# Trainium2, one core: several edits at the end of a retrieval kernel — an earlier fence, a tile of its own, half of a one-hot build on VectorE, the last rows by halves

## The chip, the cores and the metric

One NeuronCore of one Trainium2 chip runs the whole program. Its engines are named here as in the profile: PE is TensorE (matmuls), PEld its weight loads, DVE is VectorE, ACT is ScalarE, POOL is GpSimd, and SP is SyncE, which here only issues DMAs. Each engine works through its own instructions in the order in which the program gives them, and waits on semaphores for the others. The metric is the device time of one execution in microseconds (us). The time of the kernel before is the median of three executions; the profile is of one further execution.

## The reference

The program is one step of one decoder layer, for 512 prompt tokens and 32 sample tokens of width 1024. A mixer (retention heads beside a convolution) and a layer norm come first; they are not touched by the change. Then comes a product-key expert layer, and a last layer norm:

```python
q = (xb @ w_query).reshape(PEER_BLOCK, PEER_HEADS, PEER_DQ)          # 8 heads
s1 = jnp.einsum('phd,hkd->phk', q1, sub_keys_1)                      # 128 keys each
...
idx = e1 * N_KEYS + e2                                               # 16 of 16384 experts per head
gate = jax.nn.softmax(sv.astype(jnp.float32), axis=-1)
u = jnp.take(peer_u, idx, axis=0)
act = jax.nn.gelu(jnp.einsum('phkd,pd->phk', u, xb), approximate=False)
vv = jnp.take(peer_v, idx, axis=0)
return jnp.einsum('phk,phkd->pd', gate * act, vv)
...
x = layer_norm(ALPHA * x + ffn, ln2_g, ln2_b)
```

Each token thus picks 8 x 16 = 128 experts out of 16384. An expert is a row of peer_u and a row of peer_v, 1024 numbers each in float32.

## The kernel before

The 544 tokens are ordered as chunk 0 (128 prompt tokens), 32 sample tokens ("s"), chunk "b" (128 prompt tokens), and 256 prompt tokens that remain. The expert layer is done in two ways at the same time.

**By gathering** (chunk 0, then "s", then "b"). `gather`, lines 582 to 605, runs over slots. For each slot POOL issues an indirect DMA that brings 128 expert rows (8 KB each, 1 MB in all) into a buffer `g` (line 587); DVE multiplies the first half of each row with the token's x1 and sums it up, which is the *dot* (line 590); ACT applies the gelu and the gate (lines 598 and 599); DVE adds the weighted second half to `acc` (line 604). Chunk 0 and chunk "b" have 128 slots each. "s" packs four heads' shares of its 32 tokens onto 128 partitions and has 32 slots. The buffers `g` come from a pool of three, and in the slots with k % 4 == 3 of a long chunk from one more pool. `finish` (line 607) adds the scaled x1, applies the last norm and writes the chunk out, over SP's queue. `x1g`, the tile with the x1 of the chunk at hand, is one buffer that "s" and "b" use in turn (line 1006); it is loaded over ACT's queue from a copy in DRAM.

**Densely** (the other 256 tokens, `ND`). Here every expert is computed. The 16384 experts are sorted into 128 *keys* of 128 experts (the key is e2, the place within it e1). For a key, `scores_of` (line 808) loads 512 KB of peer_u over SP into a buffer `uv` (a pool of four) and makes 128 experts x 256 tokens of scores with eight matmuls, 16 records of line 815 in the profile. The gelu of them is multiplied by a gate matrix G. `v_products` (line 927) then multiplies G by a 512 KB row block of peer_v, which `v_row` (line 922) loads into the same four buffers: for each half `b` of the 256 tokens two matmuls into the two PSUM banks pB[b][0] and pB[b][1], four records of line 930 per half and row. `v_stage` (line 966) is one row for both halves.

The gate matrices are built from one-hot matrices in `build` (line 886), in units of TB = 8 tokens, 32 units in a pass. For a unit ACT makes A, which is 1 where e1 equals the row number: eight instructions that take the absolute difference (`off`, line 893) and one that takes relu(1 - x) (line 895). DVE makes M, the same comparison for e2 (line 897), and the products B of M with the gates in three bf16 parts (line 901). PE multiplies A by B, 24 matmuls per unit (line 906). A, M and B have two buffers each. The first pass (`first_keys`, line 934) builds keys 0 to 95 in groups of four tokens, and DVE multiplies the result into the scores that stand there already, or copies it where the scores come later (lines 945 and 947). The second pass (`last_keys`, line 959) builds keys 96 to 127 in groups of 16 tokens, which ACT copies out (line 963). Its target Gd takes the room of Gb, so that it can't be written before rows 0 to 31 are done.

**The order.** A planner puts the instructions of each engine in an order, by simulating them: earlier in the program text means higher priority, but an instruction that is ready is taken before one that isn't. `behind(ins, other)` (line 166) adds an order between two instructions of one engine. The following are set by hand around the change:

- In `first_keys` eight rows (`AHEAD`) are loaded and used for the first half, each behind the matmuls of a later group of tokens (`marks`).
- `first_keys` returns its last multiply; it is the *fence* (line 1019). Dots of "s" from slot FREE = 20 on, and all dots of "b", stand behind it on DVE (line 595).
- `run` (line 1021) takes one step of `phases` and two slots of `fetched` in turn. `phases` (line 971) does the second half of rows 4 to 7, which are still in their buffers, then of rows 0 to 3, which it loads again, then rows 8 to 31, the second pass with rows from 32 on, the scores of the last keys in between, and the rows up to 123. The last four rows are loaded together; line 995 does all of them for half 0 and then for half 1, in the program text. No `behind` holds this order.
- At the end two layer norms read the halves from PSUM (line 1024).

Of the kernel before, what the change touches and what calls it, by code (L numbers as in the profile page):

```python
# [8 lines left out]
F32 = mybir.dt.float32  # L9
F32R = mybir.dt.float32r  # L10
BF = mybir.dt.bfloat16
# [3 lines left out]
AF = mybir.ActivationFunctionType  # L15
# [79 lines left out]
def tile_step(ctx: ExitStack, tc: tile.TileContext, a, o):  # L95
# [508 lines left out]
                V.scalar_tensor_tensor(acc, v, wgt, acc, op0=OP.mult, op1=OP.add)  # L604
            yield

    def finish(x1, f, n, dsts, t, table=False):

        for q in range(2):
            c = slice(q * 512, (q + 1) * 512)  # L610
            V.scalar_tensor_tensor(t[:n, c], x1[:n, c], ALPHA, f[q][:n], op0=OP.mult, op1=OP.add)
        layer_norm(t, n, ln2[0], ln2[1], table=table)
        for p0, p1, dst in dsts:
            nc.sync.dma_start(dst, t[p0:p1])

    def run(*gens):

# [19 lines left out]
        Ig[g] = per.tile([128, PH // r_ * TK], I32, name=f"I{g}")  # L637
    e1T = per.tile([128, ND], F32, name="e1T")
    e2T = per.tile([128, ND], BF, name="e2T")
    gtT = per.tile([128, 3, ND], BF, name="gtT")  # L640


# [193 lines left out]
    for g in range(2):  # L836
        ef = eg[:, g].rearrange("p h k -> p (h k)")
        ei = rp.tile([128, 128], I32, name="ei")
        V.tensor_copy(ei, ef)
        V.tensor_scalar(ei, ei, NK - 1, None, op0=OP.bitwise_and)  # L840
        e1 = rp.tile([128, 128], F32, name="e1")
        V.tensor_copy(e1, ei)
        e2 = rp.tile([128, 128], F32, name="e2")
        V.tensor_sub(e2, ef, e1)
        V.tensor_scalar(e2, e2, 1.0 / NK, None, op0=OP.mult)
        p = mmps().rearrange("p (q t) -> p q t", q=4)
        for q, t in enumerate((e1, e2, eg[:, 2 + g].rearrange("p h k -> p (h k)"))):
            T.transpose(p[:, q], t, ident)
        gr = rp.tile([128, 128], F32, name="e2")
        S.activation(gr, p[:, 2], AF.Copy)  # L850
        cs = slice(g * 128, (g + 1) * 128)
        S.activation(e1T[:, cs], p[:, 0], AF.Copy, scale=-1.0)
        S.activation(e2T[:, cs], p[:, 1], AF.Copy)
        for q in range(3):
            V.tensor_copy(gtT[:, q, cs], gr)
            if q < 2:
                V.tensor_sub(gr, gr, gtT[:, q, cs])
# [28 lines left out]
    def build(bt, e0, ne, nt):  # L886


        pt = None
        for t1 in range(0, ND, TB):  # L890
            off = bt.tile([128, TB, NK], BF, name="off", bufs=1)
            for t in range(TB):
                S.activation(off[:, t], row, AF.Abs, bias=e1T[:, t1 + t:t1 + t + 1])  # L893
            A = bt.tile([128, TB, NK], BF, name="A")
            S.activation(A, off, AF.Relu, bias=1.0, scale=-1.0)  # L895
            M = bt.tile([128, TB // 2, ne, 2], BF, name="M")
            V.tensor_tensor(M, iot[:, e0:e0 + ne].unsqueeze(1).to_broadcast([128, TB // 2, ne, 2]),
                            pairs_of(e2T, t1).to_broadcast([128, TB // 2, ne, 2]), op=OP.is_equal)
            B = bt.tile([128, 3, TB // 2, ne, 2], BF, name="B")
            for q in range(3):  # L900
                V.tensor_tensor(B[:, q], M, pairs_of(gtT[:, q], t1).to_broadcast([128, TB // 2, ne, 2]), op=OP.mult)  # L901
            for t in range(t1, t1 + TB):
                if t % nt == 0:
                    pt = pdn.tile([128, nt, ne], F32, name="mm")
                for q in range(3):
                    mm = T.matmul(pt[:, t % nt], A[:, t - t1], B[:, q, (t - t1) // 2, :, t % 2], start=(q == 0),  # L906
                                  stop=(q == 2))
                if t % nt == nt - 1:
                    yield pt, slice(t - nt + 1, t + 1), mm
# [24 lines left out]
    def first_keys():  # L934

        with tc.tile_pool(name="bt", bufs=2, reuse_waits="tile") as bt:
            done = 0
            for pt, ts, mm in build(bt, 0, E0S[3], 4):
                for g, e0, e1, ready in ((0, 0, EG[0], True), (2, 0, EG[2], True), (1, 0, done, True), (1, done, EG[1], False)):
                    if e0 == e1:  # L940
                        continue
                    to = GW[g][:, e0:e1, ts]
                    part = pt[:, :, E0S[g] + e0:E0S[g] + e1].rearrange("p t e -> p e t")
                    if ready:
                        last = V.tensor_mul(to, to, part)
                    else:
                        V.tensor_copy(to, part)  # L947
                if ts.stop % 12 == 0 and done < EG[1]:
                    s_stage(E0S[1] + done, ts.stop)
                    done += 1  # L950
                if ts.stop >= 192 and ts.stop % 8 == 0:
                    marks.append(mm)
            for mm in marks[:AHEAD]:
                ahead.append(v_row(len(ahead)))
                for p in v_products(len(ahead) - 1, ahead[-1], 0):
                    behind(p, mm)
        return last

    def last_keys():

# [8 lines left out]
            v_products(e, vt, b)  # L969

    def phases():
        for e in [*range(AHEAD - UV, AHEAD), *range(AHEAD - UV)]:
            v_products(e, ahead[e] if e >= AHEAD - UV else v_row(e), 1)
            yield
        for e in range(len(ahead), EG[0]):
            v_stage(e)
            yield
        gbs.close()
        gd = ctx.enter_context(tc.tile_pool(name="gd", bufs=1, side="right", reuse_waits="tile"))
# [14 lines left out]
        ends = [(e, v_row(e)) for e in range(NK - UV, NK)]  # L994
        for b in range(2):
            for e, vt in ends:
                v_products(e, vt, b)
                yield

    def fetched():  # L1000
        t = dn.tile([128, D], F32, name="yt")
        finish(x1_0, [acc0[:, 0:512], acc0[:, 512:]], 128, [(0, 128, o[0][0, 0:128])], t)
        yield
        for g, c0, dst in (("s", 0, o[1].rearrange("b i d -> (b i) d")), ("b", NS, o[0][0, 128:256])):
            w_, r_ = GSP[g]
# [68 lines left out]
```

## Time and profile before

| what | us |
|---|---|
| median of 3 executions (1558.17 to 1561.06) | 1560.78 |
| the profiled execution, whole time | 1557.44 |
| the profiled execution, span of the trace | 1555.7 |
| granted TensorE clock, mean | 0.983 |
| PE busy | 1484.1 |
| DVE busy | 1227.7 |
| ACT busy | 581.4 |
| POOL busy | 369.6 |

The span is the time from the first to the last instruction that the profiler saw. Times in the trace count from its start. A line such as L930 is a line of the kernel before; a name such as `pB<-uv,Gd` gives the tile that is written and those that are read. "Idle before" an instruction is the time in which its engine did nothing, and the arrow names what ended it. PE's matmuls are pipelined, and their ends are modelled: a busy PE may hold short waits, and these show at PEld, the weight loads. The trace moves 505.85 MB by DMA.

### The profile page before, as it was taken

Reading aid. Unit: us, or ns where it says so; the run is one execution under the profiler, and the core shown is the slowest. Engines: PE = TensorE matmul, PEld = TensorE weight load, DVE = VectorE, ACT = ScalarE, POOL = GpSimd, SP = SyncE. Lnnn points to the kernel's source line nnn. Section 1 sums busy time; section 2 is a strip of 40 time slices with the busy share of each in tenths; the row PEclk is TensorE's granted clock in tenths of the full one; section 3 lists DMA queues with packets and bytes.
Section 4 is the critical chain, followed back from the end, with each engine's and each line's share of the span. In section 5 each row is a group of like instructions: output and inputs, shape, how many; then the busy total and the mean of one; then the engine's idle time right before and its main releaser. Section 6 shows DMA issues by size and latency. Waiting matters only on the chain.

```text
span 1555.7 us, 20736 instructions
## 1 busy us (share of the span) xinstructions
PE 1484.1 (95%) x7046; PEld 1004.1 (65%) x7046; DVE 1227.7 (79%) x3151; ACT 581.4 (37%) x1633; POOL 369.6 (24%) x329
## 2 busy tenths in 40 slices
PE   6999999897999999999999999999999999999997
PEld 6978667565866668788888884444566555543333
DVE  4779998978747999999978988666777777766664
ACT  2224453125112333333534898426992111111110
POOL 2001225322312222312231101222223222322210
PEclk9999999998999999999999999999999999999999
DMA  9648787985688779999999624999999999999993
GB/s 362 243 153 353 252 297 257 347 334 206 226 339 341 273 260 363 358 330 346 366 382 360 240 88 177 394 350 402 347 372 394 423 424 424 424 424 424 424 410 121
DMA packets 100119, 505.85 MB, mean 325 GB/s; under 512 B 10247, under 2 KB 21255, under 8 KB 57125
## 3 DMA queue, kind: packets, MB, share of 16 engines
q0 software_dynamic: 42240, 305.12, 50.4%
q1 hardware_dynamic: 51325, 192.05, 32.4%
q10 hardware_dynamic: 6448, 7.36, 1.5%
q8 instruction: 55, 0.90, 0.2%
q14 instruction: 51, 0.42, 0.1%
HBM read 499.12 MB, written 5.80 MB: 325 GB/s over the span
## 4 chain that ended last, share of the span: by engine, by line
PE 55%; DVE 20%; DMA 12%; issue 9%; POOL 3%; ACT 2%; DVEq 0%; SPq 0%; POOLq 0%; ACTq 0%
PE pB L930 27%; PE sp L815 11%; DMA g<-in_uv_dram,I 6%; PE mm L199 5%; PE mm L486 5%; DVE acc L604 4%; DVE g L590 4%; PE mm L906 3%; POOL g L587 2%; DMA g<-in_uv_dram,Is 2%; DMA g<-in_w_in_dram 2%; DMA uv<-in_uv_dram 1%; PE mm L310 1%; DVE B L901 1%; DVE score L516 1%
## 5 line engine op out<-in xcount | busy, mean ns | idle before, releaser
L815 PE MATMUL sp<-x1T,uv 128*128 128x256 f32 x2048 | 464.1, 383 | 5.2 <-DMA uv<-in_ut_dram 2.8
L604 DVE SCALAR_TENSOR_TENSOR acc<-g,wgt,acc 128x1024 f32<-128x1024 f32 x285 | 364.5, 1279 | 102.0 <-ACT wgt L599 100.4
L815 PEld LDWEIGHTS sp<-x1T,uv 128*128 128x128 f32 x2048 | 384.7, 191 | 78.5 <-issue 28.2
L598 ACT ACTIVATE act<-act 128x1 f32<-128x1 f32 x288 | 57.8, 201 | 625.7 <-DVE g L590 625.4
L587 POOL DMA_INDIRECT g<-in_uv_dram,I x128 | 166.9, 1304 | 460.1 <-DVE acc L604 259.2
L590 DVE SCALAR_TENSOR_TENSOR g<-g,x1g 128x1024 f32<-128x1024 f32 x160 | 195.2, 1222 | 71.8 <-DMA g<-in_uv_dram,Ib 50.5
L587 POOL DMA_INDIRECT g<-in_uv_dram,Ib x128 | 140.6, 1098 | 442.0 <-DVE acc L604 293.7
L199 PE MATMUL mm<-x1T,w 128*128 128x384 f32 (+1 forms) x512 | 178.3, 504 | 1.5 <-ACT score L535 1.2
L590 DVE SCALAR_TENSOR_TENSOR g<-g,x 128x1024 f32<-128x1024 f32 x128 | 154.8, 1214 | 31.0 <-DMA g<-in_uv_dram,I 30.9
L930 PE MATMUL pB<-uv,Ga 128*128 128x512 f32 x352 | 162.1, 604 | 0.2
L893 ACT ACTIVATE off<-row,e1T 128x128 bf16<-128x128 bf16 x512 | 158.0, 388 | 1.0
L199 PEld LDWEIGHTS mm<-x1T,w 128*128 128x128 f32 x512 | 97.4, 192 | 73.7 <-issue 40.3
L930 PE MATMUL pB<-uv,Gb 128*128 128x512 f32 x256 | 113.5, 597 | 4.9 <-DMA uv<-in_uv_dram 4.5
L930 PEld LDWEIGHTS pB<-uv,Ga 128*128 128x128 f32 x352 | 63.7, 189 | 83.4 <-issue 63.1
L930 PE MATMUL pB<-uv,Gd 128*128 128x512 f32 x256 | 115.5, 599 | 0.8
L930 PEld LDWEIGHTS pB<-uv,Gd 128*128 128x128 f32 x256 | 46.7, 190 | 69.7 <-issue 69.5
L930 PEld LDWEIGHTS pB<-uv,Gb 128*128 128x128 f32 x256 | 47.4, 190 | 60.7 <-issue 52.9
L906 PEld LDWEIGHTS <-A 128*128 128x128 bf16 x1536 | 60.5, 96 | 31.3 <-issue 21.3
L901 DVE TENSOR_TENSOR B<-M,gtT 128x768 bf16<-128x768 bf16 (+1 forms) x192 | 69.4, 416 | 9.4 <-PE mm L906 9.2
L930 PE MATMUL pB<-uv,Gc 128*128 128x512 f32 x160 | 72.8, 600 | 0.0
L895 ACT ACTIVATE A<-off 128x1024 bf16<-128x1024 bf16 x64 | 67.4, 1053 | 9.3 <-PE mm L906 8.5
L906 PE MATMUL mm<-B,A 128*128 128x96 bf16 (+1 forms) x1536 | 63.9, 191 | 7.3 <-DVE Gc L947 6.5
(274 smaller groups left out, 1675.4 us busy)
## 6 DMA issues: line engine op xcount, KB each, us to landing
uv<-in_uv_dram SPq DMA_DIRECT2D x132, 512.0 KB
uv<-in_ut_dram SPq DMA_DIRECT2D x128, 512.0 KB
w<-in_w_in_dram SPq DMA_DIRECT2D x18, 1024.0 KB
w<-in_w_query_dram SPq DMA_DIRECT2D x16, 1024.0 KB
w<-in_w_out_dram SPq DMA_DIRECT2D x7, 1024.0 KB
g<-in_uv_dram,I POOLq DMA_INDIRECT x128
keys<-in_state_retention_dram ACTq DMA_DIRECT2D x4, 512.0 KB
out_dram<-keys SPq DMA_DIRECT2D x4, 512.0 KB
```

What stands on the lines that cost most here:

```text
L199: T.matmul(p[:, :n], w[m // 2][:, k, (m % 2) * 128:(m % 2 + 1) * 128], xT[:, k, c0:c0 + n], start=(k == 0), stop=(k == 7))
L486: last = T.matmul(banks_[q][:n, s * 256:(s + 1) * 256], src[:, k, c0:c0 + n], wo[q * 2 + s][:, k0 + k, :], start=(xT is None and k0 == 4 a ...
L587: G.indirect_dma_start(out=t, out_offset=None, in_=a["uv"], in_offset=bass.IndirectOffsetOnAxis(ap=idx[:, k:k + 1], axis=0))
L590: dot = V.scalar_tensor_tensor(t[:, :D], t[:, :D], 1.0, x1, op0=OP.mult, op1=OP.mult, accum_out=act[:, 0:1])
L598: S.activation(act[:, 1:2], act[:, 0:1], AF.Gelu)
L604: V.scalar_tensor_tensor(acc, v, wgt, acc, op0=OP.mult, op1=OP.add)
L815: T.matmul(sp[:, i], u[:, k], x1T[:, k, NG2:], start=(k == 0), stop=(k == 7), skip_group_check=True)
L893: S.activation(off[:, t], row, AF.Abs, bias=e1T[:, t1 + t:t1 + t + 1])
L895: S.activation(A, off, AF.Relu, bias=1.0, scale=-1.0)
L901: V.tensor_tensor(B[:, q], M, pairs_of(gtT[:, q], t1).to_broadcast([128, TB // 2, ne, 2]), op=OP.mult)
L906: mm = T.matmul(pt[:, t % nt], A[:, t - t1], B[:, q, (t - t1) // 2, :, t % 2], start=(q == 0), stop=(q == 2))
L930: ps_.append(T.matmul(pB[b][q], W[:, b * 128:(b + 1) * 128], vt[:, q * 512:(q + 1) * 512], start=False, stop=(e == NK - 1), skip_group_che ...
```

## The change

- **Fence.** `first_keys` puts the last multiply of the token group that ends at 240 into `fence`, and not that of the group that ends at 256. Four groups of four tokens come after it.
- **Rows 0 to 3.** `phases` no longer does their second half right after rows 4 to 7. They are loaded again one by one after the rows 8, 9, 10 and 11, each followed by its second half.
- **x1 of chunk "b".** It gets a tile of its own in the place of chunk 0's x1 (`x1_0`), which is free by then. Its load is issued in the program text at slot FREE + 4 = 24 of "s".
- **Outputs of "s" and "b"** leave over ACT's queue.
- **A by comparisons.** In the second pass (`e0` is not 0 there) the units with an odd number get A from one DVE comparison of 8 x 128 elements, `row` against `e1B`. `e1B` is a bf16 copy of e1, which ACT writes once per 128 tokens.
- **Last rows by halves.** The products of the last four rows for half 1 stand behind the last product of half 0.

```diff
-    def finish(x1, f, n, dsts, t, table=False):
+    def finish(x1, f, n, dsts, t, table=False, q=nc.sync):
...
-            nc.sync.dma_start(dst, t[p0:p1])
+            q.dma_start(dst, t[p0:p1])
...
+    e1B = per.tile([128, ND], BF, name="e1B")
...
+        S.activation(e1B[:, cs], p[:, 0], AF.Copy)
...
         for t1 in range(0, ND, TB):
-            off = bt.tile([128, TB, NK], BF, name="off", bufs=1)
-            for t in range(TB):
-                S.activation(off[:, t], row, AF.Abs, bias=e1T[:, t1 + t:t1 + t + 1])
             A = bt.tile([128, TB, NK], BF, name="A")
-            S.activation(A, off, AF.Relu, bias=1.0, scale=-1.0)
+            if e0 and t1 // TB % 2:
+                V.tensor_tensor(A, row.unsqueeze(1).to_broadcast([128, TB, NK]),
+                                e1B[:, t1:t1 + TB].unsqueeze(2).to_broadcast([128, TB, NK]), op=OP.is_equal)
+            else:
+                off = bt.tile([128, TB, NK], BF, name="off", bufs=1)
+                for t in range(TB):
+                    S.activation(off[:, t], row, AF.Abs, bias=e1T[:, t1 + t:t1 + t + 1])
+                S.activation(A, off, AF.Relu, bias=1.0, scale=-1.0)
...
                 if ts.stop >= 192 and ts.stop % 8 == 0:
                     marks.append(mm)
+                if ts.stop == 240:
+                    fence.append(last)
...
-        return last
...
     def phases():
-        for e in [*range(AHEAD - UV, AHEAD), *range(AHEAD - UV)]:
-            v_products(e, ahead[e] if e >= AHEAD - UV else v_row(e), 1)
+        for e in range(AHEAD - UV, AHEAD):
+            v_products(e, ahead[e], 1)
             yield
-        for e in range(len(ahead), EG[0]):
+        for e in range(AHEAD, EG[0]):
             v_stage(e)
+            if e < 2 * AHEAD - UV:
+                v_products(e - AHEAD, v_row(e - AHEAD), 1)
             yield
...
         for b in range(2):
             for e, vt in ends:
-                v_products(e, vt, b)
+                ps_ = v_products(e, vt, b)
+                if b:
+                    for p in ps_:
+                        behind(p, last)
+                else:
+                    last = ps_[-1]
                 yield
...
-            x1g = dn.tile([128, D], F32, name="x1g")
-            for b in range(r_):
-                nc.scalar.dma_start(x1g[b * w_:(b + 1) * w_], x1_dram[c0:c0 + w_])
+            if g == "s":
+                x1g = dn.tile([128, D], F32, name="x1g")
+                for b in range(r_):
+                    nc.scalar.dma_start(x1g[b * w_:(b + 1) * w_], x1_dram[c0:c0 + w_])
+            else:
+                x1g = x1b
             ac = per.tile([128, D], F32, name="acc")
-            yield from gather(x1g, Ig[g], GTg[g].rearrange("p h k -> p (h k)"), ac, range(128 // r_))
+            for k, _ in enumerate(gather(x1g, Ig[g], GTg[g].rearrange("p h k -> p (h k)"), ac, range(128 // r_))):
+                if g == "s" and k == FREE + 4:
+                    x1b = per.tile([128, D], F32, name="x1_0")
+                    nc.scalar.dma_start(x1b, x1_dram[NS:NS + 128])
+                yield
...
-            finish(x1g, [ac[:, 0:512], ac[:, 512:]], w_, [(0, w_, dst)], t, g == "b")
+            finish(x1g, [ac[:, 0:512], ac[:, 512:]], w_, [(0, w_, dst)], t, g == "b", nc.scalar)
...
-    fence.append(first_keys())
+    first_keys()
```

More of the change, by code (lines that the diff above doesn't have):

```diff
@@ L605, in gather @@
             yield
-    def finish(x1, f, n, dsts, t, table=False):
-        for q in range(2):
-            c = slice(q * 512, (q + 1) * 512)
-            V.scalar_tensor_tensor(t[:n, c], x1[:n, c], ALPHA, f[q][:n], op0=OP.mult, op1=OP.add)
+    def finish(x1, f, n, dsts, t, table=False, q=nc.sync):
+        for h in range(2):
+            c = slice(h * 512, (h + 1) * 512)
+            V.scalar_tensor_tensor(t[:n, c], x1[:n, c], ALPHA, f[h][:n], op0=OP.mult, op1=OP.add)
         layer_norm(t, n, ln2[0], ln2[1], table=table)
         for p0, p1, dst in dsts:
-            nc.sync.dma_start(dst, t[p0:p1])
+            q.dma_start(dst, t[p0:p1])
     def run(*gens):
```

## The prediction

> **What bounds the kernel now.** The page comes first: who is busy, and what the chain that ended last is made of.
>
> ```profile
> span 1555.7 us, 20736 instructions
> PE 1484.1 (95%) x7046; PEld 1004.1 (65%) x7046; DVE 1227.7 (79%) x3151; ACT 581.4 (37%) x1633; POOL 369.6 (24%) x329
> PE 55%; DVE 20%; DMA 12%; issue 9%; POOL 3%; ACT 2%; DVEq 0%; SPq 0%; POOLq 0%; ACTq 0%
> ```
>
> These are averages; the change touches only what comes after about 950 us. So the second view is the busy time of each engine by stretch, cut where the work changes: end of the first build pass, plain key rows, second build pass, rows mixed with scores, last rows. Columns: stretch, length, busy us (instructions) of PE, PEld, DVE, ACT, POOL, granted clock, DMA share, GB/s.
>
> ```profile
> 958.00:983.50 25.50, 20.96 (x137) 10.20 (x138) 18.22 (x41) 17.04 (x51) 7.25 (x6) 1.00 0.89 351
> 983.50:1063.00 79.50, 79.06 (x184) 34.80 (x185) 50.93 (x64) 18.35 (x56) 20.09 (x20) 1.00 0.95 373
> 1063.00:1206.00 143.00, 142.75 (x1040) 86.48 (x1039) 106.00 (x211) 107.86 (x319) 42.73 (x33) 1.00 0.97 375
> 1206.00:1512.00 306.00, 301.51 (x835) 151.60 (x834) 214.79 (x270) 49.62 (x187) 82.34 (x81) 1.00 1.02 424
> 1512.00:1546.00 34.00, 34.00 (x80) 14.74 (x78) 12.77 (x19) 2.83 (x7) 0.00 (x0) 1.00 0.43 150
> ```
>
> TensorE has no gap worth naming from 983 to 1546, so it sets the end; only 958 to 983 is loose (20.96 of 25.50). The price of one key-row matmul comes from the second line, where nothing else runs on PE: 79.06 us for 184 records, 0.43 us each; a whole row has 8 records, 3.44 us. The fourth line has the DMA at its limit, 424 GB/s. What that costs PE is in the waits of that stretch and of 957 to 985 (waiting line, released by: us in total, times, longest):
>
> ```profile
> PEld pB L930 <- DMA uv<-in_uv_dram: 20.0, 38, 0.9
> ```
>
> ```profile
> PE pB L930 <- DMA uv<-in_uv_dram: 4.5, 4, 1.8
> PE pB L930 <- DVE Gb L945: 0.5, 1, 0.5
> ```
>
> The first view is 1206 to 1512: 20.0 us lost while POOL issued 81 gathers (its 81 instructions there are all gathers), so a gather that runs beside key rows costs PE 20.0/81 = 0.25 us, no more. The second is 957 to 985: four waits for rows, 4.5 us. Last, the tail, on VectorE and on PE:
>
> ```profile
> 1524.39 1.28 DVE L466 SCALAR_TENSOR_TENSOR yt<-yt,lrs,lnb 128x1024 f32<-128x1024 f32 x1
> 1543.85 0.70 DVE L452 BATCH_NORM_STATS2 lst<-pB 128x6 f32<-128x512 f32 x1 [18.17 <-PE pB L930]
> 1544.71 0.70 DVE L452 BATCH_NORM_STATS2 lst<-pB 128x6 f32<-128x512 f32 x1 [0.16 <-PE pB L930]
> ...
> 1547.56 0.68 DVE L452 BATCH_NORM_STATS2 lst<-pB 128x6 f32<-128x512 f32 x1
> ...
> 1551.22 1.41 DVE L466 SCALAR_TENSOR_TENSOR g<-g,lrs,lnb 128x512 f32<-128x512 f32 x2
> ```
>
> ```profile
> 1504.66 41.73 PE L930 MATMUL pB<-uv,Gd 128*128 128x512 f32 x95
> ```
>
> PE ends at 1546.39. VectorE works without a break from 1543.85 to 1552.63 on the two final norms. The last gathered chunk is ready at 1525.67, 20 us before PE: the gather side has slack, and gather slots count only by what they cost PE.
>
> **The change, part by part.**
>
> *Last keys by halves: gain 1.5.* The first half's second bank is complete at 1544.7, where the second statistics instruction was released, four records (1.72 us) before PE's end. With all eight second-half records (4 rows x 2 banks) forced behind the last first-half product, the first half is complete 8 x 0.43 = 3.44 us before the end, at 1542.95, and its first bank one record earlier, at 1542.5. The norms' 8.8 us can then start 1.3 us earlier; the lower bound for the end is PE's end plus one norm (1547.56 to 1552.63 minus the part of the first norm in between: about 4 us), 1550.3. Gain between 1.3 and 2.3, less if the order on VectorE leaves a gap; I take 1.5.
>
> *Rows 0 to 3 woven into rows 8 to 11: gain 2.0.* Today rows 0 to 3 are read again and used for one half each, back to back:
>
> ```profile
> 958.05 7.13 PE L930 MATMUL pB<-uv,Gb 128*128 128x512 f32 x16 [0.46 <-DVE Gb L945]
> 965.02 0.18 PE L906 MATMUL mm<-B,A 128*128 128x32 bf16 x1
> 967.00 1.98 PE L930 MATMUL pB<-uv,Gb 128*128 128x512 f32 x4 [1.80 <-DMA uv<-in_uv_dram]
> ...
> 971.81 1.98 PE L930 MATMUL pB<-uv,Gb 128*128 128x512 f32 x4 [0.64 <-DMA uv<-in_uv_dram]
> ...
> 975.48 1.99 PE L930 MATMUL pB<-uv,Gb 128*128 128x512 f32 x4 [0.97 <-DMA uv<-in_uv_dram]
> ...
> 979.21 3.70 PE L930 MATMUL pB<-uv,Gb 128*128 128x512 f32 x8 [1.08 <-DMA uv<-in_uv_dram]
> ...
> 983.35 77.07 PE L930 MATMUL pB<-uv,Gb 128*128 128x512 f32 x179
> ```
>
> Each brings 4 records (1.72 us) per 512 KB, and rows land some 3.7 us apart (971.8, 975.5, 979.2). Put whole rows between them, in the order 8, 0, 9, 1, 10, 2, 11, 3, and let the landings stay 967.0, 969.2, 971.8, 975.5, 979.2, then every 3.7 us. PE then does row 8 from 967.0 to 970.4, row 0 to 972.2, row 9 to 975.6, row 1 to 977.3, waits to 979.2, and so on to 992.0 after row 3. Today the same eight rows end after row 11: 983.35 plus three rows of 3.44, 993.7. Gain 1.7; if rows land as fast as PE takes them (as after 983), up to the whole 4.5 less the first 1.8, some 2.7; nothing if the earlier gathers below take the bandwidth. I take 2.0. SP issues the same loads in another order; four fewer steps stand before the second pass, which moves gather slots only.
>
> *Dots released at token 240: loss 0.9 on PE.* The end of the first pass on VectorE:
>
> ```profile
> 953.64 0.22 DVE L945 TENSOR_TENSOR Gc<-Gc,mm 128x76 f32<-128x76 f32 x1
> ...
> 953.86 1.48 DVE L901 TENSOR_TENSOR B<-M,gtT 128x768 bf16<-128x768 bf16 x3
> ...
> 957.12 0.29 DVE L945 TENSOR_TENSOR Gb<-Gb,mm 128x128 f32<-128x128 f32 x1 [0.27 <-PE mm L906]
> ...
> 958.31 1.22 DVE L590 SCALAR_TENSOR_TENSOR g<-g,x1g 128x1024 f32<-128x1024 f32 x1
> 959.46 1.22 DVE L590 SCALAR_TENSOR_TENSOR g<-g,x1g 128x1024 f32<-128x1024 f32 x1
> 960.60 1.22 DVE L590 SCALAR_TENSOR_TENSOR g<-g,x1g 128x1024 f32<-128x1024 f32 x1
> 962.15 1.27 DVE L604 SCALAR_TENSOR_TENSOR acc<-g,wgt,acc 128x1024 f32<-128x1024 f32 x1
> ```
>
> The fence moves from 958.39 to the multiply at 953.64, 4.5 us earlier. But those 4.5 us are full of build work, with one hole of 0.27. Three dots are waiting. The planner fills holes, so I expect one dot in this one: it pushes the multiplies of tokens 252 and 256 by 1.22 - 0.27 = 0.95 us, and row 4's second half on PE waits for just those (0.5 us already). Bounds: nothing, if no dot slips in; three dots and their sums, 3 x (1.22 + 1.27) = 7.5, if the planner puts all ahead. I take 0.9. In return the first refill gather starts 1 to 3 us earlier into an idle DMA: one slot.
>
> *x1b in its own place, output on ACT's queue.* The second chunk's dots wait today for the first chunk's end:
>
> ```profile
> 1011.61 0.94 POOL L587 DMA_INDIRECT g<-in_uv_dram,Ib  x1 [3.12 <-DVE acc L604]
> ...
> 1028.29 1.18 POOL L587 DMA_INDIRECT g<-in_uv_dram,Ib  x1 [5.16 <-ACT act L598]
> ```
>
> ```profile
> 1020.00:1030.00 10.00, 10.00 (x25) 4.47 (x24) 8.58 (x14) 2.77 (x9) 3.05 (x3) 1.00 0.73 246
> ```
>
> No gather is issued for 16.7 us. With x1b there the dots can fill VectorE's holes, but the first chunk's norm still takes its 9 us of VectorE; one to three slots are won. PE shows no gap there (10.00 of 10.00). SP loses a wait behind the output; PE waits for no row there, so that is worth nothing. The added load and the e1B copies (two 128x128 copies on ACT in the retrieval long before, with ACT 37% busy over the span) I put at nothing; uncovered, they cost a 128x128 ACT instruction each, 0.39 us (below).
>
> *Every other unit's A on VectorE.*
>
> ```profile
> L893 ACT ACTIVATE off<-row,e1T 128x128 bf16<-128x128 bf16 x512 | 158.0, 388 | 1.0
> L895 ACT ACTIVATE A<-off 128x1024 bf16<-128x1024 bf16 x64 | 67.4, 1053 | 9.3 <-PE mm L906 8.5
> ```
>
> ```profile
> L897 DVE TENSOR_TENSOR M<-iot,e2T 128x256 bf16<-128x256 bf16 x24 | 6.4, 285 | 0.2
> ```
>
> ```profile
> L897 DVE TENSOR_TENSOR M<-iot,e2T 128x768 bf16<-128x768 bf16 x23 | 12.5, 548 | 0.1
> ```
>
> Sixteen of the second pass's 32 units leave ACT: 16 x (8 x 0.31 (158.0/512) + 1.05) = 56 us off an ACT that has 107.86 busy in 143 us of that stretch. They arrive on VectorE as 16 compares of 1024 elements. [...] I take 1.22, since one operand (e1B) is repeated along the innermost axis, which M's pairs avoid: 19.5 us on a VectorE with 106 of 143 busy. ACT's relief speeds the gathers (33 in 143 us, 4.3 us each, against 306/81 = 3.8 later); VectorE's load slows them. With both bounds: minus 8 slots (19.5/2.5 us of dot and sum) to plus 5. I take plus one. PE's own build matmuls wait next to nothing there (142.75 of 143 busy) and keep two buffers of A; I put their cost at nothing, up to 3 us if a late gather holds VectorE ahead of an A.
>
> [...]
>
> *Sum.* Three slots won in all, 3 x 0.25 = 0.8. So -1.5 - 2.0 - 0.8 + 0.9 = -3.4 us. The profiled execution took 1557.44 (span 1555.7 and 1.74 around it), 3.3 below the median of 1560.78, and would take 1554.0; against the median that is 1557.4.
>
> **Rivals.** A difference of 0.2% (3.1 us) is what a measurement of this kernel can tell from no change.
>
> 1. *The bandwidth, not the order, limits 958 to 993.* Refill gathers and rows then share a DMA at 0.89 to 1.00; woven rows still land 3.7 us apart and PE waits the same 4.5. For it: the DMA is saturated once gathers restart. Against: whole rows give PE twice the work per byte. Result -1.4, 1559.4: no change.
> 2. *Dots ahead of the build (slower).* The planner puts the three dots and their sums ahead of the last multiplies. Price: 7.5 us at 958, directly on PE; it decides once two dots with their sums slip in (5 us, more than the other parts bring). For it: dots of the first 20 slots did interleave with the build earlier. Against: build work is traced first, and VectorE has one hole. Result -1.5 - 2.0 - 0.8 + 7.5 = +3.2, 1564.0.
> 3. *VectorE becomes the bound of the second pass.* 106 + 19.5 = 125.5 of 143 us; the gathers fall eight slots back (+2.0) and late A's hold PE 3 us. Result -1.5 - 2.0 + 0.9 + 2.0 + 3 = +2.4, 1563.2: no change, at its edge.
> 4. *Everything fits.* No dot hurts, gathers start into the idle DMA and the waits at 967 to 979 go entirely: -2.0 - 4.5 - 1.5 = -8.0, 1552.8.
>
> **How the numbers follow.** Forecast 0.45 (0.35 faster, 0.10 no change, since 3.4 lies beside the bound); rival 1 0.20 (no change); rival 2 0.15 (0.12 slower, 0.03 no change); rival 3 0.08 (0.03 slower, 0.05 no change); rival 4 0.12 (faster). Together: faster 0.47, no change 0.38, slower 0.15. The range runs from just below rival 4, 1552, to rival 2 at 1564, with up to 1 us for the spread of the median.
>
> **What would show it.** Right: PE's row waits after 965 come to under 3 us; the first half's statistics start near 1.3 us earlier before PE's end; no hole without gathers near 1011 to 1028; compares of about 1.2 us. Wrong: PE waiting more than 2 us for line 945 at the end of the first pass; build matmuls of the second pass waiting for A or B; the row waits unchanged; or a stretch from 1206 on that loses less or more than 0.25 us per gather.

## The result and the profile after

The changed kernel takes 1579.37 us (median of six runs, 1569.88 to 1584.76); the kernel before took 1559.51 beside it. The ratio is 1.0125, with a 95% interval of 1.0102 to 1.0148: **slower by 19.9 us**. The forecast was 1557.4 within 1552 to 1565, so the sign was wrong and the time lies far outside the range.

The profiled run of the changed kernel took 1584.76 us, the longest of the six and 5.4 us above their median, so the pieces below add up to more than 19.9 us. From its page, the span and the first row of busy times:

```profile
span 1583.0 us, 20611 instructions
PE 1496.1 (95%) x7046; PEld 1009.3 (64%) x7046; DVE 1246.4 (79%) x3167; ACT 530.5 (34%) x1491; POOL 391.4 (25%) x329
```

PE does the same 7046 records and is busy 12 us longer. So nearly half of the 27.3 us between the two spans (1583.0 and 1555.7) is not waiting but the same work taking longer. The stretches of 10 us around the end of the first build pass show both. First before, then after (columns as in the prediction; PEclk is the last but two):

```profile
960.00:970.00 10.00, 8.20 (x35) 3.68 (x34) 7.44 (x17) 7.13 (x23) 3.17 (x4) 1.00 0.88 322
970.00:980.00 10.00, 7.31 (x69) 3.73 (x68) 5.94 (x16) 5.40 (x15) 0.94 (x1) 1.00 1.01 422
980.00:990.00 10.00, 10.00 (x47) 4.71 (x46) 6.37 (x14) 9.72 (x30) 3.35 (x2) 1.00 0.99 384
```

```profile
960.00:970.00 10.00, 6.18 (x53) 3.59 (x50) 10.00 (x29) 6.78 (x19) 0.00 (x0) 0.90 0.01 2
970.00:980.00 10.00, 8.39 (x24) 4.07 (x22) 9.61 (x23) 6.44 (x19) 8.25 (x4) 0.59 0.71 252
980.00:990.00 10.00, 3.74 (x54) 2.11 (x52) 1.35 (x3) 0.26 (x2) 1.87 (x2) 0.93 0.93 335
990.00:1000.00 10.00, 8.16 (x61) 4.28 (x61) 8.42 (x19) 7.84 (x23) 2.62 (x2) 0.73 0.74 284
```

After, PE loses 3.8, 1.6, 6.3 and 1.8 us in the four stretches, and beside that the granted clock falls: 0.59 over ten microseconds is 8.2 of them at half clock ((1 - 0.59) x 2 x 10). The trace's record of the clock, which has no granted share but 1.00 and 0.50, stands at 0.50 (half clock) from 968.0 for 10.2 us and from 988.5 for 6.8 us; the kernel before has none between 925 and 1549.

What held PE is seen in its waits from 955 to 1010. (Lines from the second half of `build` on are six higher in the changed kernel: L906 is L912, L930 is L936, L945 is L951.)

```profile
PE mm L912 <- DVE B L907: 8.1, 1, 8.1
PE mm L912 <- DVE Gc L951: 3.4, 1, 3.4
PE pB L936 <- DVE Gb L951: 1.6, 1, 1.6
PE mm L912 <- DVE Gc L953: 0.8, 2, 0.5
```

The waits for rows, 4.5 us before, are gone, but 13.9 us of waits for VectorE stand in their place. (A build matmul writes into a PSUM tile `mm`; it has to wait until the multiplies of an earlier token group, Gc the last of them, have read that tile.) The timeline of VectorE tells the first of them:

```profile
962.94 1.49 DVE L907 TENSOR_TENSOR B<-M,gtT 128x768 bf16<-128x768 bf16 x3
964.34 1.22 DVE L590 SCALAR_TENSOR_TENSOR g<-g,x1g 128x1024 f32<-128x1024 f32 x1
...
965.48 1.22 DVE L590 SCALAR_TENSOR_TENSOR g<-g,x1g 128x1024 f32<-128x1024 f32 x1
...
966.63 1.22 DVE L590 SCALAR_TENSOR_TENSOR g<-g,x1g 128x1024 f32<-128x1024 f32 x1
...
969.28 1.28 DVE L604 SCALAR_TENSOR_TENSOR acc<-g,wgt,acc 128x1024 f32<-128x1024 f32 x1
...
971.07 1.28 DVE L604 SCALAR_TENSOR_TENSOR acc<-g,wgt,acc 128x1024 f32<-128x1024 f32 x1
972.27 0.28 DVE L951 TENSOR_TENSOR Gb<-Gb,mm 128x128 f32<-128x128 f32 x1
```

All three waiting dots stand directly ahead of the multiplies of the last four token groups, and two sums among those multiplies. The last multiply of Gb, which row 4's second half needs, starts at 972.27, that is 30.0 us after the first row product. Before, it started at 957.72, 24.6 us after it, and the three dots stood behind it:

```profile
957.72 0.28 DVE L945 TENSOR_TENSOR Gb<-Gb,mm 128x128 f32<-128x128 f32 x1
```

On PE, and again on VectorE twenty microseconds later:

```profile
968.92 2.08 PE L912 MATMUL mm<-B,A 128*128 128x96 bf16 x24 [3.37 <-DVE Gc L951]
972.61 9.94 PE L936 MATMUL pB<-uv,Gb 128*128 128x512 f32 x16 [1.60 <-DVE Gb L951]
982.38 1.35 PE L912 MATMUL mm<-B,A 128*128 128x32 bf16 x48
991.81 1.15 PE L912 MATMUL mm<-B,A 128*128 128x32 bf16 x24 [8.07 <-DVE B L907]
```

```profile
988.44 1.23 DVE L590 SCALAR_TENSOR_TENSOR g<-g,x1g 128x1024 f32<-128x1024 f32 x1 [8.31 <-DMA g<-in_uv_dram,Is]
990.27 1.28 DVE L604 SCALAR_TENSOR_TENSOR acc<-g,wgt,acc 128x1024 f32<-128x1024 f32 x1 [0.60 <-ACT wgt L599]
991.47 0.69 DVE L907 TENSOR_TENSOR B<-M,gtT 128x256 bf16<-128x256 bf16 x3
```

The sixteen row products that took 7.13 us before take 9.94, the first of them at half clock, which lasts until 978.2. Then a dot waits 8.31 us for its gather, the B behind it on VectorE waits with it, the build matmul waits for that B, and the rows stand behind the build matmul on PE: that is the second hold.

The tail is the one place where the changed kernel is better. Before, VectorE's statistics of the two halves stood nearly back to back behind PE; now the first half's are done long before:

```profile
1568.32 0.70 DVE L452 BATCH_NORM_STATS2 lst<-pB 128x6 f32<-128x512 f32 x1 [39.68 <-PE pB L936]
...
1575.19 0.70 DVE L452 BATCH_NORM_STATS2 lst<-pB 128x6 f32<-128x512 f32 x1 [2.10 <-PE pB L936]
```

To put the pieces beside each other, this table counts from the first row product of each kernel, since what lies ahead differs from run to run: the first transpose of the gates on PE (line 848), which no edit touches, starts between 645.0 and 658.8 us in the profiles, at 648.1 before and 654.7 after. All are starts and ends of row-product records in the trace; the two kernels at the right are experiments below.

| us | before | after | held multiplies (e6) | fence alone (e5) |
|---|---|---|---|---|
| first row product | 933.2 | 942.2 | 935.1 | 936.5 |
| row 4's second half starts | +24.9 | +30.4 | +29.5 | +29.2 |
| rows 4 to 7 done | +32.0 | +40.3 | +38.3 | +37.8 |
| rows 0 to 3 and 8 to 11 done | +60.7 | +73.8 | +66.7 | +68.9 |
| last row product ends | +613.2 | +633.8 | +619.7 | +623.7 |
| from there to the end of the span | 9.3 | 7.0 | 9.3 | 9.3 |

So of the 27.3 us, 9.0 lie ahead of the first row product (6.6 of them already at that transpose), 13.1 between it and row 11, 7.5 after that, and 2.3 come back in the tail.

### The profile page after: what moved, and what is told of

The parts are those of the page before. It is cut to its first block, busy times and chain, and to the rows that moved or that the text cites. A ratio compares the mean times of both kernels' runs of the same rounds, so it can differ in the third digit from the quotient of the medians.

```text
span 1583.0 us, 20611 instructions
## 1 busy us (share of the span) xinstructions
PE 1496.1 (95%) x7046; PEld 1009.3 (64%) x7046; DVE 1246.4 (79%) x3167; ACT 530.5 (34%) x1491; POOL 391.4 (25%) x329
## 4 chain that ended last, share of the span: by engine, by line
PE 35%; DMA 24%; DVE 22%; issue 13%; POOL 4%; ACT 2%; SPq 0%; DVEq 0%; POOLq 0%; ACTq 0%
PE pB L936 15%; DMA g<-in_uv_dram,Ib 12%; DVE acc L604 6%; DMA g<-in_uv_dram,I 5%; PE mm L199 5%; PE mm L486 5%; PE sp L816 4%; DVE g L590 4%; DMA g<-in_uv_dram,Is 4%; POOL g L587 3%; PE mm L912 2%; DMA g<-in_w_in_dram 2%; DVE B L907 1%; PE mm L310 1%; DVE iu L515 1%
## 5 line engine op out<-in xcount | busy, mean ns | idle before, releaser
L590 DVE SCALAR_TENSOR_TENSOR g<-g,x 128x1024 f32<-128x1024 f32 x256 | 311.4, 1220 | 88.9 <-DMA g<-in_uv_dram,Ib 53.4
L587 POOL DMA_INDIRECT g<-in_uv_dram,Ib x128 | 155.5, 1215 | 342.0 <-DVE acc L604 240.7
L936 PE MATMUL pB<-uv,Ga 128*128 128x512 f32 x352 | 162.5, 605 | 0.4 <-DMA uv<-in_uv_dram 0.2
L936 PE MATMUL pB<-uv,Gb 128*128 128x512 f32 x256 | 119.0, 617 | 3.5 <-DMA uv<-in_uv_dram 1.7
L900 ACT ACTIVATE off<-row,e1T 128x128 bf16<-128x128 bf16 x384 | 117.7, 388 | 3.6 <-PE mm L912 2.6
L936 PEld LDWEIGHTS pB<-uv,Ga 128*128 128x128 f32 x352 | 63.4, 189 | 84.5 <-issue 63.1
L936 PE MATMUL pB<-uv,Gd 128*128 128x512 f32 x256 | 113.7, 597 | 1.6 <-DMA uv<-in_uv_dram 1.0
L587 POOL DMA_INDIRECT g<-in_uv_dram,Is x32 | 43.5, 1358 | 194.3 <-DVE acc L604 172.3
L936 PEld LDWEIGHTS pB<-uv,Gd 128*128 128x128 f32 x256 | 47.3, 190 | 67.9 <-issue 55.1
L936 PEld LDWEIGHTS pB<-uv,Gb 128*128 128x128 f32 x256 | 48.4, 196 | 65.2 <-issue 53.0
L912 PEld LDWEIGHTS <-A 128*128 128x128 bf16 x1536 | 61.3, 97 | 43.9 <-issue 21.1
L912 PE MATMUL mm<-B,A 128*128 128x96 bf16 (+1 forms) x1536 | 65.4, 192 | 20.6 <-DVE B L907 8.1
L936 PE MATMUL pB<-uv,Gc 128*128 128x512 f32 x160 | 75.2, 614 | 0.0
L199 PE MATMUL mm<-g,w 128*128 128x160 f32 (+1 forms) x512 | 67.7, 288 | 1.6 <-DMA w<-in_w_in_dram 1.3
```

What stands on the lines that cost most here:

```text
L199: T.matmul(p[:, :n], w[m // 2][:, k, (m % 2) * 128:(m % 2 + 1) * 128], xT[:, k, c0:c0 + n], start=(k == 0), stop=(k == 7))
L587: G.indirect_dma_start(out=t, out_offset=None, in_=a["uv"], in_offset=bass.IndirectOffsetOnAxis(ap=idx[:, k:k + 1], axis=0))
L590: dot = V.scalar_tensor_tensor(t[:, :D], t[:, :D], 1.0, x1, op0=OP.mult, op1=OP.mult, accum_out=act[:, 0:1])
L936: ps_.append(T.matmul(pB[b][q], W[:, b * 128:(b + 1) * 128], vt[:, q * 512:(q + 1) * 512], start=False, stop=(e == NK - 1), skip_group_che ...
```

## The experiments

Each ratio is against the kernel before on the same chip, with its 95% interval; microseconds in brackets are worked out from it (times 1560).

**e1: the changed kernel with the fence back at the last multiply.**

```diff
-                if ts.stop == 240:
-                    fence.append(last)
...
+        return last
...
+    fence.append(first_keys())
```

> The changed kernel with the fence back at token 256, all else as changed. Theory 1 (the early fence: three dots stand ahead of the last four groups' multiplies on VectorE, PE waits 3.4 and 1.6 us for them, idles, and its granted clock halves behind that) expects most of the 20 us back: 1562 to 1570 us. Theory 2 (the comparisons on VectorE: a late gather holds the B of the second pass, PE waits 8.1 us for line 907) expects 1574 to 1577, the 5 us of the dots alone.

Measured: 1556.29 us, ratio 0.9977, 0.9951 to 1.0003 (-3.6 us, -7.6 to +0.5). The loss is gone entirely, which is more than the first theory expected. No half clock stands between 810 and 1550. PE's waits from 955 to 1012 are 0.9 us for Gc, 0.5 for Gb, none for B, and for rows

```profile
PE pB L936 <- DMA uv<-in_uv_dram: 2.4, 2, 1.7
```

Rows 0 to 3 and 8 to 11 are done 58.5 us after the first row product, 2.2 less than before. So the fence is needed for the loss.

**e2: the changed kernel with all A's on ACT as before.**

```diff
-            if e0 and t1 // TB % 2:
-                V.tensor_tensor(A, row.unsqueeze(1).to_broadcast([128, TB, NK]),
...
-            else:
...
+            off = bt.tile([128, TB, NK], BF, name="off", bufs=1)
```

> The changed kernel with every A made on ScalarE again (no e1B, no comparison on VectorE). Theory 2 (comparisons) expects 8 us or more back: 1565 to 1572, and no wait of PE for B above 2 us near the end of the first pass. Theory 1 (fence) expects the dots still ahead of the multiplies and the time within 4 us of the changed kernel's 1579.

Measured: 1574.7 us, ratio 1.0091, 1.0056 to 1.0127 (+14.2, 8.7 to 19.8). Without one comparison on VectorE most of the loss is there (the time lies just below the 1575 us at which the band of the first theory begins, and above that of the second); PE still waits 3.4 us for Gc, 1.6 for Gb and 4.7 for B.

**e3: the changed kernel with rows 0 to 3 done right after rows 4 to 7, as before.**

```diff
+        for e in [*range(AHEAD - UV, AHEAD), *range(AHEAD - UV)]:
+            v_products(e, ahead[e] if e >= AHEAD - UV else v_row(e), 1)
```

> The changed kernel with rows 0 to 3 again right behind rows 4 to 7. If the woven rows help as predicted (2 us), this is 1 to 4 us slower than the changed kernel: 1580 to 1583. If they do harm (second-pass matmuls that wait for B now stand ahead of whole rows), it is 3 to 8 us faster: 1571 to 1576.

Measured: 1575.34 us, ratio 1.0099, 1.0062 to 1.0135 (+15.4, 9.7 to 21.1). Most of the loss is there with the old order of the rows, and so are the waits: 3.4 for Gc, 1.6 for Gb and 7.1 for B. The time lies where the expectation put a harm done by the woven rows, 4 us below the changed kernel, but its interval reaches past the 19.9 us of that kernel; whether the woven rows add to the loss beside the holds is not settled.

**e4: the changed kernel with x1 of chunk "b" in the shared tile, as before.**

```diff
+            x1g = dn.tile([128, D], F32, name="x1g")
+            for b in range(r_):
+                nc.scalar.dma_start(x1g[b * w_:(b + 1) * w_], x1_dram[c0:c0 + w_])
```

> The changed kernel with the second chunk's x1 again in the shared tile x1g, loaded when the first chunk is done. By the price of 0.25 us per gather it should be within 2 us of the changed kernel. The theory that the early gathers take bandwidth from the rows before the second pass (PE lost 7 us more between 1016 and 1100) expects 4 to 8 us back: 1571 to 1575, and a gap of the gathers near 1030.

Measured: 1567.49 us, ratio 1.0054, 1.0033 to 1.0075 (+8.4, 5.1 to 11.7). About 11 us of the loss go with this tile, more than either reading expected. In its waits the first hold is left (3.4 for Gc), the second is not there: no wait for B at all, and rows are waited for again (4.9 us). So the tile's part lies in the second hold, or ahead of it.

**e5: the kernel before with the fence at 240 and nothing else.**

```diff
+                if ts.stop == 240:
+                    fence.append(last)
...
-        return last
...
-    fence.append(first_keys())
+    first_keys()
```

> The kernel before with the fence moved to token 240 and nothing else. Theory (the early dots are the cause, whatever else changes): the dots stand in DVE's order ahead of the multiplies of the last four token groups here too, so TensorE waits at the end of the first pass, its granted clock halves behind the wait, and the time rises by 12 to 20 us, a ratio of 1.008 to 1.013. Rival (the dots hurt only together with the woven rows and the comparisons, which need VectorE there): the time rises by less than 4 us, a ratio under 1.0025.

Measured: 1569.35 us, ratio 1.0056, 1.0033 to 1.008 (+8.7, 5.1 to 12.5). Less than the theory's 12 to 20, more than the rival's 4. The three dots stand ahead of the multiplies here too, PE waits 3.4 us for Gc, and half clock follows (6.8 us from 961.9; 3.4 more from 979.0, behind a wait of 3.8 for a row). The fence alone slows the kernel, but by the middle of its interval it makes less than half of the loss.

**e6: the kernel before, fence at 256, the last multiplies held by idle work.** Five VectorE instructions that change no value stand between the multiplies of tokens 240 and 244.

```diff
+                if ts.stop == 240:
+                    for g in (2, 0, 2, 0, 2):
+                        x = GW[g][:, :, 240:256]
+                        d = V.scalar_tensor_tensor(x, x, 1.0, x, op0=OP.mult, op1=OP.max)
+                        behind(d, last)
+                    last = d
```

> The kernel before, fence at token 256, with five idle VectorE instructions between the multiplies of token 240 and 244 (the maximum of Ga or Gb with itself over the last 16 tokens, 3136 elements a partition, about 3.7 us in all, the length of three dots). No dot or gather starts earlier, and no sum comes between the multiplies. Theory (a held TensorE costs the wait and then its clock): a half-clock stretch of 6.8 to 10.2 us appears behind the wait, and the time rises by 3.7 plus half of the stretch, 7 to 9 us, a ratio of 1.0045 to 1.006. Rival 1 (the wait alone counts): plus 3 to 4 us and no half-clock stretch, 1.002 to 1.0025. Rival 2 (the earlier gathers and the late dot that holds B are the price, the multiplies' delay is hidden): within 2 us.

Measured: 1565.39 us, ratio 1.0042, 1.0017 to 1.0067 (+6.6, 2.7 to 10.5). PE's largest waits from 950 to 1010, and the stretch that follows:

```profile
PE mm L906 <- DVE Gc L945: 3.7, 1, 3.7
PE pB L930 <- DMA uv<-in_uv_dram: 3.1, 3, 1.4
```

```profile
960.00:970.00 10.00, 7.43 (x33) 4.35 (x34) 8.81 (x24) 5.11 (x18) 1.90 (x1) 0.66 0.23 77
```

One hold of 3.7 us is followed by 6.8 us of half clock (0.66 is (1 - 0.66) x 2 x 10 = 6.8 us). Wait and clock together are 3.7 + 3.4 = 7.1 us, and the last row product ends 6.5 us later against the first than before. Nothing is gathered earlier in this kernel. That is the theory's case, with a median just under its 7 to 9 us. Its lower interval end alone would not shut out the plain wait, but the clock record does.

**e7: the kernel before with x1 of chunk "b" in its own tile and nothing else.**

```diff
+                if g == "s" and k == FREE + 4:
+                    x1b = per.tile([128, D], F32, name="x1_0")
+                    nc.scalar.dma_start(x1b, x1_dram[NS:NS + 128])
```

> The kernel before with x1 of chunk b in its own tile, loaded at slot 24 of s, and nothing else. Theory (this edit delays the first pass): the first row product of the first half starts 5 to 8 us later than in the kernel before, at 938 to 941 us, and the time rises by 4 to 8 us, a ratio of 1.0025 to 1.005. Rival (the late start in the two kernels with this edit came with the comparisons' copies of e1 or from the spread of the retrieval): within 2 us of the kernel before, 0.999 to 1.0013, or a little faster by one to three gather slots.

Measured: 1566.06 us (1549.55 to 1569.43), ratio 1.0028, 0.9999 to 1.0056 (+4.4, -0.2 to 8.7): not settled. The first row product did come late, at 944.1. But 5.1 us of that are clock: 13.7 us at half clock in the first pass against 3.4 before, and the longest stretch stands behind a wait of 3.6 us for a block of peer_u at 797. Pauses of 2.5 to 5.2 us between 789 and 809 stand in ten of the fourteen profiles, with this tile and without it, and e9, which has the tile, starts at 935.0. So the late start can't be put down to the tile. From the first row product on, e7 is as before (+24.9, +60.7, +611.9).

**e8: the kernel before with the woven rows and the halves and nothing else.**

```diff
+            if e < 2 * AHEAD - UV:
+                v_products(e - AHEAD, v_row(e - AHEAD), 1)
...
+                if b:
+                    for p in ps_:
+                        behind(p, last)
```

> The kernel before with the woven rows 0 to 3 and the last rows by halves, and nothing else. Theory (their gains are real and independent of the rest): minus 2.0 to 2.2 for the rows and minus 1.5 to 2.4 for the tail, together 3.5 to 4.6 us faster, a ratio of 0.9970 to 0.9978. Rival (the woven rows gain only because the later gathers of the changed kernel leave them the bandwidth): only the tail's 1.5 to 2.4 us, 0.9985 to 0.999.

Measured: 1556.94 us, ratio 0.9979, 0.996 to 0.9997 (-3.3, -6.2 to -0.5): faster, by what both readings allow. The waits from 955 to 1003 say more:

```profile
PE pB L930 <- DMA uv<-in_uv_dram: 1.8, 1, 1.8
PE mm L906 <- DVE B L901: 1.2, 1, 1.2
```

The waits for rows fell from 4.5 to 1.8 us. But a B is now late by 1.2 us, with 3.4 us of half clock behind it, and rows 8 to 11 are done at +61.3, no earlier than before. With the fence at 256 and the comparisons (e1, e10) this B is not late. In this profile, of the longest of the twelve runs, the gain is given back by a smaller case of the same loss.

**e9: the kernel before with the fence at 240 and the tile of its own, nothing else** (the edits of e5 and e7 together).

```diff
+                if ts.stop == 240:
+                    fence.append(last)
...
+                    x1b = per.tile([128, D], F32, name="x1_0")
```

> The kernel before with the fence at token 240 and x1 of chunk b in its own tile, and nothing else. Theory (these two edits together make the second hold: a dot that waits for its gather stands in VectorE's order ahead of a B of the second pass, and TensorE waits 5 to 8 us for that B with its clock halved behind it): plus 14 to 20 us against before, a ratio of 1.009 to 1.013, and a wait of TensorE for B of over 4 us between 975 and 1005. Rival (the two only add up, 9.6 and 4 us or less): plus 9 to 13 us, a ratio of 1.006 to 1.0085, and no such wait.

Measured: 1576.55 us, ratio 1.013, 1.011 to 1.0151 (+20.3, 17.2 to 23.6). These two edits give the whole loss of the changed kernel (1.0125). PE's two largest waits from 955 to 1012:

```profile
PE mm L906 <- DVE B L901: 4.8, 1, 4.8
PE mm L906 <- DVE Gc L945: 3.4, 1, 3.4
```

Both holds are there. A long wait for B (4.7 to 8.1 us) stands in all four kernels that have both edits and in none that has one of them.

**e10: the changed kernel without these two edits** (fence at 256, shared tile; woven rows, halves, ACT's queue and comparisons stay; the edits of e1 and e4 together).

```diff
-                if ts.stop == 240:
-                    fence.append(last)
...
-                    x1b = per.tile([128, D], F32, name="x1_0")
```

> The changed kernel without the fence at 240 and without the tile for x1 of chunk b: woven rows, halves, outputs over ACT's queue and comparisons stay. Theory (the two edits taken out are the ones that cost): 3.5 to 6 us faster than before, a ratio of 0.996 to 0.9978, and the first row product starts before 937 us. Rival (the comparisons cost by themselves what the other edits bring): within 2 us of before, 0.9985 to 1.0013.

Measured: 1556.84 us, ratio 0.9982, 0.9959 to 1.0004 (-2.8, -6.4 to +0.6). Between the two readings. The first row product starts at 938.2, a little later than the 937 that the theory allowed. From there it is 2.3 us ahead at row 11 (+58.5), level at the last row product (+613.0), and 2.3 ahead in the tail (7.0). The outputs over ACT's queue are in this kernel, which is no slower than before; they have no experiment of their own.

**e11: the kernel before with the comparisons and nothing else** (the reverse of e2, with the copy of e1).

```diff
+        S.activation(e1B[:, cs], p[:, 0], AF.Copy)
...
+            if e0 and t1 // TB % 2:
+                V.tensor_tensor(A, row.unsqueeze(1).to_broadcast([128, TB, NK]),
```

> The kernel before with every other unit's A of the second pass by VectorE comparisons, and nothing else. The prediction on record: 1.22 us for each comparison, no cost on TensorE, plus 0.25 us, a ratio of 1.0000 to 1.0005. Rival 1 (ACT's relief frees gather slots and the last build matmuls come earlier): 1 to 4 us faster, 0.9975 to 0.9995. Rival 2 (late comparisons hold TensorE): 2 to 5 us slower, 1.0013 to 1.003, with waits of TensorE for A.

Measured: 1562.46 us, ratio 1.0019, 0.999 to 1.0047 (+3.0, -1.6 to +7.3): can't be told from no change. The groups and the stretch from 1063 to 1206, first before, then this kernel:

```profile
1063.00:1206.00 143.00, 142.75 (x1040) 86.48 (x1039) 106.00 (x211) 107.86 (x319) 42.73 (x33) 1.00 0.97 375
```

```profile
1063.00:1206.00 143.00, 142.72 (x1032) 84.10 (x1031) 120.56 (x226) 68.42 (x202) 48.76 (x34) 1.00 0.96 381
```

```profile
L895 DVE TENSOR_TENSOR A<-row,e1B 128x1024 bf16<-128x1024 bf16 x16 | 19.5, 1221 | 4.7 <-PE mm L912 4.7
```

ACT falls by 39.4 us and VectorE rises by 14.6 in this stretch, the last build matmul ends at 1156.9 instead of 1171.5, and PE is as busy as before: there was nothing for it to gain. No build matmul waits for an A.

**e12: the kernel before with the halves and nothing else** (the second part of e8).

```diff
+                if b:
+                    for p in ps_:
+                        behind(p, last)
```

> The kernel before with the last rows by halves and nothing else. Theory: the time from the end of TensorE's last row product to the end of the span falls from 9.3 to 7.0 us, and the time falls by 1.5 to 2.4 us, a ratio of 0.9985 to 0.999. Rival (the first half's statistics wait for something else, or VectorE's order leaves a gap): less than 0.5 us, the tail stays at 9 us.

Measured: 1554.95 us, ratio 0.9995, 0.9976 to 1.0013 (-0.8, -3.7 to +2.0). The time alone doesn't tell. The tail is 7.0 us in the trace, as in every kernel with this edit (7.0 in all eight), and 9.3 in all six without it. I take the 2.3 us from there. Its rows stand in the old order, and still rows 0 to 3 and 8 to 11 are done at +59.3, with 2.7 us of waits for rows:

```profile
PE pB L930 <- DMA uv<-in_uv_dram: 2.7, 2, 1.8
```

## Why the prediction was wrong, point by point

**Dots released at token 240: the step that failed.** The prediction said: "The planner fills holes, so I expect one dot in this one", and put the loss at 0.9 of bounds from 0 to 7.5. In the program three dots went ahead of the multiplies, and two sums among them. VectorE had no hole there and stayed full (10.00 of 10.00 from 960 to 970). That the hole in the trace decides how many dots slip in was the wrong inference: the order is fixed before the kernel runs, by what the planner supposes to be ready, and the trace shows only what came of another order. The sign that the prediction itself named, PE waiting more than 2 us for line 945, came true with 3.4 us. Why the planner supposed so was not tried.

Rival 2 named this mechanism and its place, and its condition held (three dots). Its price was 7.5 us; the fence alone measured 8.7 (5.1 to 12.5). That it comes out near is partly chance, since the parts are others: PE's wait is 3.4 us for the dots and only 0.4 (e5) to 1.6 us (the changed kernel) for the sums. Much of the rest is **the clock**, which no part of the prediction has. e6 shows it by itself: 3.7 us of wait, 6.8 us of half clock, 6.5 us at the last row product.

**x1b: slots won, and no loss on PE.** In its one profile e7 shows no loss from the first row product on; beside the fence there is a loss. With both, a dot that waits for its gather stands ahead of a B that PE needs, and PE waits 4.7 to 8.1 us, again with half clock behind it. This is the sentence "up to 3 us if a late gather holds VectorE ahead of an A" of the comparisons, with B in the place of A, at the wrong edit and too low. The hole without gathers did shrink, from 16.7 us to 10.3:

```profile
1023.49 0.94 POOL L587 DMA_INDIRECT g<-in_uv_dram,Ib  x1 [2.75 <-DVE acc L604]
1033.74 4.11 POOL L587 DMA_INDIRECT g<-in_uv_dram,Ib  x1 [9.31 <-ACT acc L602]
```

How the sum of e9's parts comes about is **open**: 8.7 and 4.4 make 13.1, and 20.3 was measured. The second hold with its wait (4.8 us in e9) takes the place of 3.6 us of waits for rows (5.5 in e5, 1.9 in e9), and with its half clock rows 8 to 11 are done 2.9 us later than in e5 (+71.8 against +68.9). The rest of the 7.2 us isn't accounted for, though the intervals of e5 and e7 are wide enough to hold it. e9's one profile, of a run 6 us below its median, ends its row products only 0.7 us later than e5's. The 7.5 us that the changed kernel loses after row 11 lie for the most part in three pauses:

```profile
PE mm L912 <- ACT Gd L970: 1.8, 1, 1.8
PE pB L936 <- DMA uv<-in_uv_dram: 1.7, 1, 1.7
PE sp L816 <- ACT act L598: 1.3, 1, 1.3
```

Behind the first of these, at 1088.6, stand 3.4 us of half clock. In all PE is idle for 9.8 us there against 5.2 before, and the clock takes 1.7 more. Which edit brings these pauses was not tried.

**Rows woven: a gain as forecast, but its size is not settled.** Forecast 2.0; where nothing holds PE, e1 and e10 are at row 11 2.2 and 2.3 us sooner than before, with 2.4 and 2.3 us of waits for rows left of 4.5. But e12, in the old order, is 1.4 us sooner too, with 2.7 us of such waits; against it the gain is 0.8 to 0.9. The sign that was named for it, row waits under 3 us, is thus met without the edit. In the changed kernel it can't be seen, since the holds give the rows time to land.

**Last keys by halves: right, at its upper bound.** Forecast 1.5 of 1.3 to 2.3; it measured 2.3. The term was mis-sized: the second half of four rows was counted as eight records, but a half has four records a row, so sixteen follow, 16 x 0.43 = 6.9 us. That is what the statistics show above (1568.32 and 1575.19), and so only the second norm is left behind PE.

**Comparisons: right in the trace.** 1.22 us each were forecast and measured (1221 ns on average in e11, 1216 to 1226 in the changed kernel), no build matmul waits for them in e11, and 34 gathers in the stretch against 33 are the one slot; the time of e11 doesn't settle their cost. Ahead of the result the 1.22 us was the author's estimate, by the length of a 128x1024 dot at line 590: no row in it shows such a comparison. M's rows, 285 ns at 256 elements and 548 at 768, would make it 0.68 us at 1024; with e1B repeated along the innermost axis it took 1.22.

**The price of a gather slot: right.** 79 gathers from 1215 to 1542 in the changed kernel, and this wait in the same stretch, are 0.26 us each, against 0.25:

```profile
PEld pB L936 <- DMA uv<-in_uv_dram: 20.7, 40, 0.8
```

Together: of the parts that were forecast as gains, the rows measured 0.8 to 2.3 us and the halves 2.3, against 2.0 and 1.5; the 0.8 us for slots was not measured by itself. One step, taken at 0.9 of up to 7.5, outweighed them, because the likeliest case was chosen by a hole in the wrong order and its price held no clock.

## What to carry to other kernels

Work that is released ahead of a deadline is put there by whatever orders the queue; look at the resulting order on the engine, not at the holes of the old trace. What stands behind a released instruction on an in-order engine pays its whole length (here 1.22 us a dot), and pays for its data too if that is late (8.31 us for one gather). And where TensorE is the bound, price a wait of several microseconds with its clock: here 3.7 us of wait cost 6.6 (2.7 to 10.5).

## What the runs showed of the hardware

- **TensorE's granted clock fell to 0.50 behind its pauses.** From 690 to 1540 us in the fourteen profiles, each of the 23 pauses of PE of over 2.5 us has a stretch of half clock that starts within it or at most 1.2 us behind it and lasts 3.4, 6.8 or 10.2 us; of 63 pauses of 1.2 to 2.5 us, 18 have such a start in them or at most 2.2 us behind them. Row products start 0.85 us apart there (after, 973.62 to 977.89) against 0.43 otherwise, so such a stretch cost half its length where PE was busy.
- **This is also part of the spread between runs.** The kernel before ranged from 1549 to 1568 us over all rounds. The mean granted clock is 0.9866 in the ten fastest of its 84 recorded executions (mean 1552.0 us) and 0.9818 in the ten slowest (1565.2): by an estimate from these, 0.0048 x 1557 = 7.5 us of the 13.3 between them. Between the start of the first pass and the first row product the fourteen profiles have from 3.4 to 20.5 us at half clock, partly behind a block of peer_u that came late near 800 us, partly behind shorter waits of the build.
